# Five sevens in a row in the output product, and sums of the down weights at a period of seven steps

## The chip, the core and the metric

The kernel runs on one core of a Trainium2 chip. TensorE (PE) multiplies matrices, VectorE (DVE) and ScalarE (ACT) work on tiles in the core's memory, SyncE (SP) issues the transfers between DRAM and that memory; each engine works through its own list of instructions in order and waits on semaphores that others raise. The metric is device time in microseconds (us) of one execution: median of three runs 1462.11 us, from 1461.22 to 1462.31.

## The reference

One layer of a transformer for 256 tokens of width 2048: three kinds of attention heads, whose merged outputs go through `w_out` (2048 x 2048), and a feed-forward part whose up product has two halves of 5632 columns, each put through a causal convolution of width 3. All in float32.

```python
for l in range(DEPTH):
    h = rms_norm(x, g_mix[l])
    proj = h @ w_in[l]
    ...
    merged = (g[:, :, 0] * (o_fox @ w_br_fox[l])
              + g[:, :, 1] * (o_sb @ w_br_sb[l])
              + g[:, :, 2] * (o_mem @ w_br_mem[l]))
    x = x + merged @ w_out[l]

    h2 = rms_norm(x, g_ffn[l])
    u = causal_depthwise_conv(h2 @ w_up[l], conv_w[l], conv_b[l])
    u_gate, u_val = jnp.split(u, 2, axis=-1)
    x = x + (jax.nn.silu(u_gate) * u_val) @ w_down[l]
return x
```

The three attention branches stand in place of "..."; the change touches the products with `w_out`, `w_up` and `w_down`.

## The kernel before

Weights stream through the core in pieces of 128 x 1024 floats (512 KB). ScalarE casts each raw piece to a rounded part `hi`, VectorE subtracts to get the rest `lo`, and a product is the sum of three matmuls: x-hi by w-hi, x-lo by w-hi, x-hi by w-lo (`three`; in the up stage a matmul of 512 columns with both parts of x and one of 256 columns, L1231 and L1232). `hi` and `lo` have four buffers each, raw pieces four and, in some stages, two more.

The output and down stages (`blocked`) go through blocks of 1024 output columns. A block is a sum over pairs of 128-row slices of the weights: eight pairs in the output stage. A plan, a string, gives each pair's way:

- "e", `eight`: two slices by two halves of the tokens by two halves of the columns, eight products, 24 matmuls of 512 columns, two raw pieces.
- "s", `seven`: the same product of 2 x 2 blocks by seven products, 21 matmuls. It needs four sums of the activations (`pair_sums`, tiles `ms` in the output stage) and four sums of the weights, T1 to T4. Its loads are half a slice with T3, a whole slice, T1 with T2 as one piece (`raw_t`), and T4 (half a piece): 3.5 pieces.

The weights' sums don't depend on the activations, so they are made earlier in the kernel and kept in DRAM (`kept`). The list `halves` gives the order: the output stage's pairs first, then those of the down stage. Three streams draw from it: one in the attention stage (13 pairs, period 6), one by halves in the merged stage, and one in the up stage (`pair_sums_ahead`: period 8, sums one step behind the load, store five steps behind, starting after 22 steps). A step is one `tick`; the up stage ticks once for each piece of `w_up`. A pair of the stream is one load of 1 MB (`pre_d`), three additions on VectorE (`sums_in`, L249 to L251) and one store of 1 MB, all through one staging tile of tag "ends"; a new load waits until the last store has read the tile.

The up stage works on groups of four column tiles (`f0` = 0, 4, 8, ...; both halves `s` = 0 and 1 in turn). A group is eight pieces (`k` = 0, 2, ..., 14), 64 pairs of matmuls, into four banks. When a group is done, its four banks go through `conv` beside the next group: ScalarE copies half of a bank (L1167), VectorE adds the other half (L1168), scales it into one of two padded tiles (L1177), ScalarE applies one tap (L1182), VectorE two (L1183, L1184), and in the second half multiplies with the first half's result (L1190) and splits (L176, L177). On VectorE the pieces' `lo` are pinned to the order of the program by `pin`, the three additions by `in_order`; the convolution's rows are placed among them by a scheduler, which also sees the priorities that the program's order gives. One group of instructions on VectorE and ScalarE thus reads, as `lo_u24_0_6`, "lo of column tiles 24 to 27, half 0, slices 6 and 7".

## Time and profile before

| | |
|---|---|
| median of three runs | 1462.11 us (1461.22 to 1462.31) |
| the profiled execution | 1461.49 us, of which the span of its instructions 1459.8 |
| TensorE busy | 1454.0 us (100%), 7314 matmuls |
| VectorE busy | 1213.4 us (83%) |
| ScalarE busy | 850.0 us (58%) |
| output stage | 658 to 743 us of the span |
| up stage | 745 to 1225 us of the span |

The page's first part gives busy time per engine; the list of waits gives idle time of one engine by what it waited for; the chain goes back from the last instruction, at each step to what released it; windows give the same busy times for a stretch; timelines list single instructions with start, duration, engine, line, output and inputs, and in brackets the idle time ahead of them with what ended it. `x2` behind a row means two like instructions in one row. A duration includes a part in which the next instruction already runs: the spacing of starts is the pace.

### The profile page before, as it was taken

Reading aid. Unit: us, or ns where it says so; the run is one execution under the profiler, and the core shown is the slowest. Engines: PE = TensorE matmul, PEld = TensorE weight load, DVE = VectorE, ACT = ScalarE, POOL = GpSimd, SP = SyncE. Lnnn points to the kernel's source line nnn. Section 1 sums busy time; section 2 is a strip of 40 time slices with the busy share of each in tenths; the row PEclk is TensorE's granted clock in tenths of the full one; section 3 lists DMA queues with packets and bytes.
Section 4 is the critical chain, followed back from the end, with each engine's and each line's share of the span. In section 5 each row is a group of like instructions: output and inputs, shape, how many; then the busy total and the mean of one; then the engine's idle time right before and its main releaser. Section 6 shows DMA issues by size and latency. Waiting matters only on the chain.

```text
span 1459.8 us, 20547 instructions
## 1 busy us (share of the span) xinstructions
PE 1454.0 (100%) x7314; PEld 1230.1 (84%) x7314; DVE 1213.4 (83%) x1791; ACT 850.0 (58%) x1212; POOL 19.3 (1%) x48
## 2 busy tenths in 40 slices
PE   9999999999999999999999999999999999999998
PEld 7888888888888888888888888888888888888887
DVE  5778777776898899997887888888888877999878
ACT  6755454564564555545666556556556565676665
POOL 0000000010000000000000000000000000000000
PEclk9999999999999999999999999999999999999999
DMA  9697798777668576788877888888888866899995
GB/s 312 202 330 248 267 341 288 238 241 222 209 207 269 172 231 198 270 265 263 276 196 232 288 266 306 278 273 299 283 281 298 267 200 202 253 291 333 299 324 222
DMA packets 162534, 381.08 MB, mean 261 GB/s; under 512 B 12234, under 2 KB 27486, under 8 KB 158334
## 3 DMA queue, kind: packets, MB, share of 16 engines
q1 hardware_dynamic: 161022, 377.52, 78.9%
q10 hardware_dynamic: 1328, 2.11, 0.4%
q8 instruction: 57, 0.93, 0.3%
q14 instruction: 47, 0.39, 0.1%
q0 software_dynamic: 80, 0.13, 0.0%
HBM read 343.01 MB, written 36.70 MB: 260 GB/s over the span
## 4 chain that ended last, share of the span: by engine, by line
PE 97%; DVE 1%; DMA 1%; issue 0%; SPq 0%; ACT 0%; DVEq 0%; ACTq 0%
PE u L1231 22%; PE u L1232 11%; PE xd L329 3%; PE xd L330 3%; PE xd L328 3%; PE xg L330 3%; PE xg L329 3%; PE xg L328 3%; PE s L328 2%; PE s L330 2%; PE f L330 2%; PE f L328 2%; PE f L329 2%; PE s L329 2%; PE b L330 2%; PE b L328 2%
## 5 line engine op out<-in xcount | busy, mean ns | idle before, releaser
L1231 PE MATMUL u<-hT,hi_u 128*128 128x512 f32 x1232 | 428.3, 394 | 0.0
L1232 PE MATMUL u<-hT,lo_u 128*128 128x256 f32 x1232 | 341.3, 277 | 0.0
L1231 PEld LDWEIGHTS u<-hT,hi_u 128*128 128x128 f32 x1232 | 231.0, 188 | 53.8
L143 DVE TENSOR_TENSOR lo_u<-raw_u,hi_u 128x1024 fp32r<-128x1024 f32 x176 | 215.1, 1222 | 73.2 <-ACT hi_u L142 71.9
L142 ACT CAST hi_u<-raw_u 128x1024 fp32r<-128x1024 f32 x176 | 184.7, 1050 | 135.0 <-PE u L1231 106.7
L1232 PEld LDWEIGHTS u<-hT,lo_u 128*128 128x128 f32 x1232 | 231.2, 188 | 0.0
L323 DVE TENSOR_TENSOR lo_d<-raw_d,hi_d 128x1024 fp32r<-128x1024 f32 x88 | 106.7, 1222 | 16.2 <-ACT hi_d L322 13.8
L322 ACT CAST hi_d<-raw_d 128x1024 fp32r<-128x1024 f32 x88 | 91.7, 1053 | 38.8 <-PE xd L329 17.8
L322 ACT CAST hi_g<-raw_g 128x1024 fp32r<-128x1024 f32 (+1 forms) x80 | 77.1, 972 | 48.9 <-PE xg L329 19.2
L323 DVE TENSOR_TENSOR lo_g<-raw_g,hi_g 128x1024 fp32r<-128x1024 f32 (+1 forms) x80 | 88.6, 1119 | 4.1 <-ACT hi_g L322 4.1
L142 ACT CAST hi_f<-raw_f 128x1024 fp32r<-128x1024 f32 (+1 forms) x40 | 38.5, 967 | 51.8 <-PE f L329 42.8
L330 PE MATMUL xg<-lo_g,xT 128*128 128x512 f32 x175 | 68.1, 389 | 0.0
L329 PE MATMUL xg<-hi_g,xT 128*128 128x512 f32 x175 | 68.1, 389 | 0.0
L328 PE MATMUL xg<-hi_g,xT 128*128 128x512 f32 x175 | 68.1, 389 | 0.0
L143 DVE TENSOR_TENSOR lo_f<-raw_f,hi_f 128x1024 fp32r<-128x1024 f32 (+1 forms) x40 | 44.6, 1118 | 22.3 <-ACT hi_f L142 21.7
L143 DVE TENSOR_TENSOR lo_s<-raw_s,hi_s 128x1024 fp32r<-128x1024 f32 (+1 forms) x40 | 44.7, 1117 | 20.9 <-ACT hi_s L142 20.9
L1231 PE MATMUL u<-hT_rest,hi_u 128*128 128x512 f32 x176 | 62.0, 394 | 0.0
L142 ACT CAST hi_b<-raw_b 128x1024 fp32r<-128x1024 f32 x32 | 33.6, 1051 | 45.2 <-DMA raw_b<-in_w_br_fox_dram 15.8
L142 ACT CAST hi_s<-raw_s 128x1024 fp32r<-128x1024 f32 (+1 forms) x40 | 38.4, 961 | 36.8 <-PE s L329 23.9
L1182 ACT ACTIVATE y<-u,taps 128x256 f32<-128x256 f32 x88 | 49.6, 596 | 16.3 <-DVE u L1177 16.2
L330 PE MATMUL xd<-lo_d,aT 128*128 128x512 f32 x148 | 57.6, 389 | 0.0
L328 PE MATMUL xd<-hi_d,aT 128*128 128x512 f32 x148 | 57.6, 389 | 0.0
(520 smaller groups left out, 3473.1 us busy)
## 6 DMA issues: line engine op xcount, KB each, us to landing
raw_u<-in_w_up_dram SPq DMA_DIRECT2D x176, 512.0 KB, 4.5
raw_g<-in_w_in_dram SPq DMA_DIRECT2D x96, 512.0 KB, 4.4
raw_d<-in_w_down_dram SPq DMA_DIRECT2D x63, 512.0 KB, 5.4
pre_d<-in_w_down_dram SPq DMA_DIRECT2D x17, 1024.0 KB, 6.2
kept_d<-pre_d SPq DMA_DIRECT2D x17, 1024.0 KB, 6.2
raw_f<-in_w_in_dram SPq DMA_DIRECT2D x32, 512.0 KB, 4.9
raw_s<-in_w_in_dram SPq DMA_DIRECT2D x32, 512.0 KB, 5.2
raw_t_d<-kept_d SPq DMA_DIRECT2D x25, 512.0 KB, 5.8
```

What stands on the lines that cost most here:

```text
L142: pin(nc.scalar.copy(hi[:, :m], raw[:, :m]))
L143: pin(nc.vector.tensor_tensor(lo[:, :m], raw[:, :m], hi[:, :m].bitcast(F32), ALU.subtract))
L322: nc.scalar.copy(hi[:, :n], src)
L323: nc.vector.tensor_tensor(lo[:, :n], src, hi[:, :n].bitcast(F32), ALU.subtract)
L328: fix(nc.tensor.matmul(o, lhsT=ah, rhs=w[0], start=first, stop=False))
L329: fix(nc.tensor.matmul(o, lhsT=al, rhs=w[0], start=False, stop=False))
L330: fix(nc.tensor.matmul(o, lhsT=ah, rhs=w[1], start=False, stop=last))
L1182: nc.scalar.activation(y, u[:, 2:], AF.Identity, scale=tap(2), bias=tap(3))
L1231: nc.tensor.matmul(ps[i], lhsT=hi[:, j, c], rhs=hT(k + j), start=first, stop=False)
L1232: nc.tensor.matmul(ps[i][:, :S], lhsT=lo[:, j, c], rhs=hT(k + j)[:, :S], start=False, stop=last)
```

## The change

Four things change together. The output stage's plans go from two eights, two sevens, one eight, two sevens, one eight to two eights, five sevens, one eight. Before, the sevens took pairs 0 to 3 and the eights 4 to 7; now the five sevens take pairs 0, 1, 2, 3 and 6 and the eights 4, 5 and 7. The activations' sums for pair 6 are made by a new generator, `last_merged_sums`, in a tile of the tag under which the heads' outputs lay. Two more pairs of `w_out` stand at the front of `halves`, so two pairs of the down stage go from the attention stage's stream to the up stage's, which now makes 19 and goes at period 7, with the sums in the step of the load and the store four steps behind. And the up stage's matmuls are pinned to the program's order.

```diff
-    o_plans = ("eessesse", "eessesse")
+    o_plans = ("eessssse", "eessssse")
...
+    o_sevens = (0, 1, 2, 3, 6)
+    pairs = lambda name, n: o_sevens if name == "o" else range(n)
...
-        for pr in range(plan.count("s"))
+        for pr in pairs(name, plan.count("s"))
...
-        s, e = 0, ns
+        s, e = 0, 0
+        sp = pairs(name, ns)
+        ep = [p for p in range(len(plan) - plan.count("f")) if p not in sp]
...
-                by_seven(s, s == 0, s == ns - 1)
+                by_seven(sp[s], s == 0, s == ns - 1)
...
-                eight(e, i == 0, i == len(plan) - 1)
+                eight(ep[e], i == 0, i == len(plan) - 1)
...
     def merged_sums():
         yield 1
-        for p in range(o_plans[0].count("s")):
+        for p in range(4):
...
+    def last_merged_sums():
+        yield 2
+        after = op.tile([P, KT, 2 * S], F32R, tag="ot", name="m_after")
+        ms[6] = after[:, 0:2].rearrange("p k c -> p (k c)").rearrange("p (f l q) -> p f l q", f=4, l=2)
+        pair_sums(mT[6], block("mw_6"), [(ms[6], slice(0, 4))])
...
+    later(last_merged_sums())
...
-        pair_sums_ahead(lambda name: ends_tile(name, F32).rearrange("p i c -> p (i c)"), 8, 1, 5, delay=DU)
+        pair_sums_ahead(lambda name: ends_tile(name, F32).rearrange("p i c -> p (i c)"), 7, 0, 4, delay=DU)
...
-                        nc.tensor.matmul(ps[i], lhsT=hi[:, j, c], rhs=hT(k + j), start=first, stop=False)
-                        nc.tensor.matmul(
-                            ps[i][:, :S], lhsT=lo[:, j, c], rhs=hT(k + j)[:, :S], start=False, stop=last
+                        in_order(nc.tensor.matmul(ps[i], lhsT=hi[:, j, c], rhs=hT(k + j), start=first, stop=False))
+                        in_order(
+                            nc.tensor.matmul(
+                                ps[i][:, :S], lhsT=lo[:, j, c], rhs=hT(k + j)[:, :S], start=False, stop=last
+                            )
```

In the changed kernel the lines behind line 236 have other numbers: L249 to L251 are L251 to L253, L1168 is L1179, L1177 is L1188, L1183 and L1184 are L1194 and L1195, L1190 is L1201, L384 is L386, L415 to L421 are L417 to L423.

What the order shows, at three places. First SyncE's queue in block 0 of the output stage: `raw_o0_5` is slice 5 of the weights, the second of pair 2; `raw_t_o0_2` is pair 2's T1 and T2, `raw_t4_o0_2` its T4. Before:

```order
L419 DMA raw_t_o0_1_6102<-kept_o0_1_1030 128x2x512
L384 DMA raw_o0_13_6161<-in_w_out_dram 128x1024
L421 DMA raw_t4_o0_2_6186<-kept_o0_2_1201 128x512
L415 DMA raw_o0_4_6179<-in_w_out_dram 128x512
L416 DMA raw_o0_4_6179<-kept_o0_2_1201 128x512
L384 DMA raw_o0_5_6182<-in_w_out_dram 128x1024
L419 DMA raw_t_o0_2_6184<-kept_o0_2_1201 128x2x512
```

and now:

```order
L421 DMA raw_t_o0_1_6102<-kept_o0_1_1030 128x2x512
L386 DMA raw_o0_5_6154<-in_w_out_dram 128x1024
L423 DMA raw_t4_o0_2_6158<-kept_o0_2_1201 128x512
L421 DMA raw_t_o0_2_6156<-kept_o0_2_1201 128x2x512
L417 DMA raw_o0_6_6197<-in_w_out_dram 128x512
L418 DMA raw_o0_6_6197<-kept_o0_3_1392 128x512
```

The pieces of the eight (12, 13) no longer stand between pairs 1 and 2; the first piece of pair 2 is issued far earlier (not shown), and its T load is three rows behind that of pair 1 instead of six.

Second, VectorE in the up stage behind `lo_u12_0_4`, the piece of column tiles 12 to 15, half 0, slices 4 and 5; `cr`, `u`, `y` and `aT` are tiles of the convolution of tiles 8 to 11. Before:

```order
L143 TENSOR_TENSOR lo_u12_0_4_8181<-raw_u12_0_4_8179,hi_u12_0_4_8180 128x1024
L1168 TENSOR_TENSOR cr_8_1_8113<-cr_8_1_8113,u8_1_7864 128x256
L1168 TENSOR_TENSOR cr_9_1_8124<-cr_9_1_8124,u9_1_7865 128x256
L1177 TENSOR_TENSOR u_0_6990<-cr_8_1_8113,rbc_5954 128x256
L1177 TENSOR_TENSOR u_1_6992<-cr_9_1_8124,rbc_5954 128x256
L143 TENSOR_TENSOR lo_u12_0_6_8203<-raw_u12_0_6_8201,hi_u12_0_6_8202 128x1024
L1183 TENSOR_SCALAR y_8_1_8117<-u_0_6990,taps_110,y_8_1_8117 128x256
```

Now the row of `lo_u12_0_4` is followed by 27 others, 24 of the convolution and the three sums, until `lo_u12_0_6`; the last twelve rows from there:

```order
L252 TENSOR_TENSOR pre_d0_10_8231<-pre_d0_10_8231 128x512
L1194 TENSOR_SCALAR y_10_1_8190<-u_0_7018,taps_110,y_10_1_8190 128x256
L1194 TENSOR_SCALAR y_11_1_8201<-u_1_7020,taps_110,y_11_1_8201 128x256
L1195 TENSOR_SCALAR y_10_1_8190<-u_0_7018,taps_110,y_10_1_8190 128x256
L1195 TENSOR_SCALAR y_11_1_8201<-u_1_7020,taps_110,y_11_1_8201 128x256
L1201 TENSOR_TENSOR y_10_0_7963<-y_10_0_7963,y_10_1_8190 128x256
L1201 TENSOR_TENSOR y_11_0_7972<-y_11_0_7972,y_11_1_8201 128x256
L253 TENSOR_TENSOR pre_d0_10_8231<-pre_d0_10_8231 128x512
L177 TENSOR_TENSOR aT_6749<-y_10_0_7963,aT_6749 128x256
L177 TENSOR_TENSOR aT_6749<-y_11_0_7972,aT_6749 128x256
L143 TENSOR_TENSOR lo_u12_0_6_8238<-raw_u12_0_6_8236,hi_u12_0_6_8237 128x1024
```

Before, four rows stood between the two lo pieces; now the whole convolution of the four banks does, with a pair's sums among it. Like runs stand behind `lo_u24_0_6` (18 rows of the convolution and the sums), `lo_u24_1_4` (16) and `lo_u28_0_2` (17).

Third, the last of these, VectorE behind `lo_u28_0_2`. Before:

```order
L143 TENSOR_TENSOR lo_u28_0_2_9953<-raw_u28_0_2_9951,hi_u28_0_2_9952 128x1024
L143 TENSOR_TENSOR lo_u28_0_4_9997<-raw_u28_0_4_9995,hi_u28_0_4_9996 128x1024
L1168 TENSOR_TENSOR cr_24_1_9929<-cr_24_1_9929,u24_1_9680 128x256
L1168 TENSOR_TENSOR cr_25_1_9940<-cr_25_1_9940,u25_1_9681 128x256
L1177 TENSOR_TENSOR u_0_6990<-cr_24_1_9929,rbc_5954 128x256
```

and now:

```order
L143 TENSOR_TENSOR lo_u28_0_2_9989<-raw_u28_0_2_9987,hi_u28_0_2_9988 128x1024
L251 TENSOR_TENSOR pre_d1_8_10010<-pre_d1_8_10010 128x1024
L252 TENSOR_TENSOR pre_d1_8_10010<-pre_d1_8_10010 128x512
L1179 TENSOR_TENSOR cr_24_1_9965<-cr_24_1_9965,u24_1_9716 128x256
L1179 TENSOR_TENSOR cr_25_1_9976<-cr_25_1_9976,u25_1_9717 128x256
L1188 TENSOR_TENSOR u_0_7018<-cr_24_1_9965,rbc_5954 128x256
```

Here two of the sums come directly behind the lo piece, the convolution of tiles 24 to 27 behind them, and `lo_u28_0_4` behind that.

## Prediction

> **What bounds the kernel now.** I read the page's shares first, then the waits of TensorE, then windows by stage, and last the timelines of VectorE and TensorE in the two stages that the change touches. Page, parts 1 and 4:

> ```profile
> span 1459.8 us, 20547 instructions
> PE 1454.0 (100%) x7314; PEld 1230.1 (84%) x7314; DVE 1213.4 (83%) x1791; ACT 850.0 (58%) x1212; POOL 19.3 (1%) x48
> PE 97%; DVE 1%; DMA 1%; issue 0%; SPq 0%; ACT 0%; DVEq 0%; ACTq 0%
> ```

> All waits of TensorE (line waited for; us in total, times, longest):

> ```profile
> PE spare L92 <- DVE qscale L531: 1.2, 1, 1.2
> PE kv L154 <- DVE memT L185: 0.5, 2, 0.2
> ```

> Both lie in the first microseconds. So the time is the sum of the matmuls: every matmul taken away shortens it, and every microsecond by which a piece of weights is late lengthens it. The windows below are the output stage, the up stage without its ends, and a piece of the down stage with five sevens in a row (busy time of each engine, granted clock, DMA share, GB/s):

> ```profile
> 658.00:743.20 85.20, 85.20 (x390) 70.75 (x389) 70.25 (x80) 53.65 (x69) 0.00 (x0) 1.00 0.82 260
> 780.00:1200.00 420.00, 420.00 (x2425) 367.17 (x2424) 361.43 (x595) 252.33 (x389) 0.00 (x0) 1.00 0.84 276
> 1421.00:1444.50 23.50, 23.50 (x106) 19.42 (x105) 20.14 (x20) 18.30 (x21) 0.00 (x0) 1.00 0.90 326
> ```

> TensorE fills each window. VectorE is 86% busy in the up stage (361.43 of 420): room on average, but only if its work comes evenly.

> **Part 1, the products.** Per block of the output stage one eight (24 matmuls) becomes a seven (21), so 6 matmuls of 512 columns go. Their spacing, from two rows that are 14 matmuls apart:

> ```profile
> 739.79 0.39 PE L328 MATMUL xo<-hi_o,mT 128*128 128x512 f32 x1
> 742.97 0.39 PE L330 MATMUL xo<-lo_o,mT 128*128 128x512 f32 x1
> ```

> 3.18 / 14 = 0.227 us each, hence **−1.36 us** (0.09%). Changes under 0.2%, 2.9 us, can hardly be told from none on this kernel; by itself this term would read as the same.

> **Part 2, five sevens in a row.** A seven brings 3.5 pieces per 21 matmuls where an eight brings 2 per 24. The third window shows the denser stream (326 GB/s, share 0.90) carried for 23.5 us without a gap on TensorE, so I cost the rate at nothing. The one transfer that moves to a tighter place is the T load of pair 2 in block 0: two pieces of an eight no longer stand ahead of it. It takes the raw slot that came free at 674.33; its nearest like, issued at 677.08, landed when its cast started at 683.33, 6.25 us later:

> ```profile
> 674.33 0.33 SPq L415 DMA_DIRECT2D raw_o<-in_w_out_dram  x1
> 677.08 0.38 SPq L419 DMA_DIRECT2D raw_t_o<-kept_o  x1
> 679.49 1.06 ACT L322 CAST hi_o<-raw_o 128x1024 fp32r<-128x1024 f32 x1 [0.30 <-PE yo L329]
> 683.33 1.05 ACT L322 CAST hi_t_o<-raw_t_o 128x1024 fp32r<-128x1024 f32 x1 [1.52 <-DMA raw_t_o<-kept_o]
> 690.78 1.83 DVE L323 TENSOR_TENSOR lo_t_o<-raw_t_o,hi_t_o 128x1024 fp32r<-128x1024 f32 x2
> 693.58 0.39 PE L330 MATMUL yo<-lo_t_o,ms 128*128 128x512 f32 x1
> ```

> 674.33 + 6.25 = 680.6, against the cast slot at 679.49: 1.1 late. The reserve is 1.57 us (lo done 692.01, read 693.58). Cost 0, bounds 0 and 1.1. Pair 6's own sums (five VectorE rows, some 2.3 us by the like operations below) fall in VectorE's idle time, the times in brackets:

> ```profile
> 668.05 1.23 DVE L323 TENSOR_TENSOR lo_t_o<-raw_t_o,hi_t_o 128x1024 fp32r<-128x1024 f32 x1 [1.33 <-ACT hi_t_o L322]
> 670.81 0.69 DVE L323 TENSOR_TENSOR lo_t_o<-raw_t_o,hi_t_o 128x512 fp32r<-128x512 f32 x1 [0.94 <-PE mt L989]
> 673.07 1.23 DVE L323 TENSOR_TENSOR lo_o<-raw_o,hi_o 128x1024 fp32r<-128x1024 f32 x1 [0.93 <-ACT hi_o L322]
> ```

> Those are 3.2 us in one stretch of six. Without that cover the sums could delay the lo pieces behind them by up to 2.3, of which the 1.57 of reserve takes most: under 1 us, inside the range.

> **Part 3, the up stage.** TensorE's order does not change here; VectorE's does. A piece of w_up takes eight pairs of L1231 and L1232, 22.2 / 8 = 2.77 us. One column group is eight pieces. At period 8 the sums of a pair (L249 to L251) keep one place in the group, behind the last lo piece, clear of the conv work. At period 7 they come one piece earlier each time, and at four pairs they run into the conv rows; there the whole run now stands ahead of a lo piece. The prices:

> ```profile
> 920.93 1.23 DVE L143 TENSOR_TENSOR lo_u<-raw_u,hi_u 128x1024 fp32r<-128x1024 f32 x1 [1.55 <-ACT hi_u L142]
> 922.10 0.77 DVE L1168 TENSOR_TENSOR cr<-cr,u 128x256 f32<-128x256 f32 x2
> 923.70 1.23 DVE L143 TENSOR_TENSOR lo_u<-raw_u,hi_u 128x1024 fp32r<-128x1024 f32 x1 [0.16 <-ACT hi_u L142]
> 924.84 0.87 DVE L1183 SCALAR_TENSOR_TENSOR y<-u,taps,y 128x256 f32<-128x256 f32 x2
> ...
> 928.77 1.22 DVE L143 TENSOR_TENSOR lo_u<-raw_u,hi_u 128x1024 fp32r<-128x1024 f32 x1
> 936.51 1.22 DVE L249 TENSOR_TENSOR pre_d<-pre_d 128x1024 f32<-128x1024 f32 x1
> 937.64 0.42 DVE L177 TENSOR_TENSOR aT<-y,aT 128x256 fp32r<-128x256 f32 x1
> 937.98 0.69 DVE L250 TENSOR_TENSOR pre_d<-pre_d 128x512 f32<-128x512 f32 x1
> 938.58 1.22 DVE L143 TENSOR_TENSOR lo_u<-raw_u,hi_u 128x1024 fp32r<-128x1024 f32 x1
> ```

> Starts give the pace: 11 conv operations from 924.84 to 928.77 are 0.357 us each. A pair's sums are 1.13 (936.51 to 937.64) + 0.60 (937.98 to 938.58) and, with the same form as L250, 0.60 again: 2.33 us. And how far ahead of TensorE a lo piece is:

> ```profile
> 922.53 0.39 PE L1231 MATMUL u<-hT,hi_u 128*128 128x512 f32 x1
> 930.86 0.39 PE L1231 MATMUL u<-hT,hi_u 128*128 128x512 f32 x1
> 931.09 0.27 PE L1232 MATMUL u<-hT,lo_u 128*128 128x256 f32 x1
> ```

> By tile numbers the lo of 923.70 is first read at 931.09, and the one of 920.93 (done 922.16) one piece, 2.77 us, before. So from the end of one lo to the need of the next there are 931.09 − 922.16 = 8.93 us, and the next lo itself takes 1.22: **7.71 us of other work fit between two lo pieces**. What the new order puts there, counted row by row:

> - A, behind lo of f12, first half, k = 4: 24 conv operations and the sums, 24 × 0.357 + 2.33 = 10.9: 3.2 late.
> - B, behind f24, first half, k = 6: 18 and the sums, 8.76: 1.05 late.
> - C, behind f24, second half, k = 4: 16 and the sums, 8.04: 0.33 late.
> - D, behind f28, first half, k = 2: 17 and the sums, 8.40: 0.7 late. Here the first two sums (1.73 us) stand right behind the lo, would end in this group at 919.38 + 1.73 = 921.1, and the first conv must wait for ScalarE's copy of the finished bank, whose first half the conv at 922.10 took: 1.0 more, 1.7.

> ```profile
> 918.15 1.23 DVE L143 TENSOR_TENSOR lo_u<-raw_u,hi_u 128x1024 fp32r<-128x1024 f32 x1 [0.68 <-ACT hi_u L142]
> 921.69 0.73 ACT L1167 COPY cr<-u 128x256 f32<-128x256 f32 x2 [0.79 <-PE u L1232]
> ```

> Sum **+6.3 us**, bounds 0 (if the lead is longer than in this group) and 9.3 (if the conv work of A, B and C waits 1.0 for ScalarE's copy too, as in D). Before, the worst run between two lo pieces was the 11 operations shown, 3.93 us, which is why nothing waits. What is late next after a stall is nothing: casts go on behind free buffers while TensorE stands.

> **Part 4, transfers of the stream.** One staging tile serves the pairs in turn: load, sums, store, next load. Issue to landing, by part 6 of the page:

> ```profile
> raw_u<-in_w_up_dram SPq DMA_DIRECT2D x176, 512.0 KB, 4.5
> pre_d<-in_w_down_dram SPq DMA_DIRECT2D x17, 1024.0 KB, 6.2
> kept_d<-pre_d SPq DMA_DIRECT2D x17, 1024.0 KB, 6.2
> ```

> Load and store are 12.4 us of 7 × 2.77 = 19.4 (before 22.2): 7.0 us remain for the sums to get done, against 9.8. Where they stand behind 8.6 us of conv work, the store slips, the next load waits on SyncE's queue, and the raw_u loads behind it wait too; with 0.84 of the DMA engines' time taken and two pairs (4 MB each way) more to move, it catches up slowly. No row shows such a slip. Bounds: 0, since raw_u lies four buffers ahead, and 5, if each of A to D hands on its whole 8.6 − 7.0 = 1.6 us with a little less. I take **1.3**, nearer to the lower end because the buffers cover a single slip of 1.6.

> **The sum.** 1461.49 − 1.36 + 6.3 + 1.3 = 1467.7 us against the profiled execution. The median of the runs stands 0.62 above that execution, so 1468.3.

> **Rivals.**
> 1. *The stalls don't come.* For it: VectorE is 14% idle, and a lead of 6.2 us is measured in one group. It decides where the work between two lo pieces stays under 7.7 us; if the lead were 11 us (the length of A), nothing would wait, and 1461.49 − 1.36 + 0.62 = 1460.8, not slower. Against it: the lead is capped by four lo buffers, and four pieces at 2.77 us are 11.1 from which the cast, the subtract and the matmuls' own use of a buffer are off. A weaker form, with A alone late, gives 1464.0.
> 2. *Transfers bind.* The slips of part 4 add up from pair to pair: 19 pairs, of which five or six hand on 1.6 us: 4 to 8 more than the forecast, 1472 to 1476. For it: DMA share 0.84, and one tile for all. Against: the third window above moved 326 GB/s, 18% more than the up stage's 276.
> 3. *The clock falls behind the longest stall.* At the program's start seven spare matmuls of 384 columns take 2.42 us, 0.346 each, twice what the spacing above gives, until about 3.8 us after the first. At the end the last matmul ends at 1455.83, and the granted clock is 1.00 up to 1459 and lower behind it:

> ```profile
> 1.23 2.42 PE L92 MATMUL spare<-idle 128*128 128x384 bf16 x7 [1.23 <-DVE qscale L531]
> 1455.55 0.28 PE L330 MATMUL apart<-lo_d,a_ends 128*128 128x256 f32 x1
> 1458.00:1459.00 1.00, 0.00 (x0) 1.00 0.00 0
> 1459.00:1459.80 0.80, 0.00 (x0) 0.56 0.04 10
> ```

> So an idle time of over 3.2 us can halve the clock for some 3.8 us, which loses half of that, 1.9 us. A is at that edge: 1470.2. [...]
> 4. *The output stage starves* with five sevens in a row: about 1 us per block, 1470.3. Against: the third window.

> That six matmuls go is certain from the order; the rest of the output stage's plan only changes places.

> **How the numbers follow.** Forecast 0.64 (1465.5 to 1471.5), rival 1 in full 0.07, in its weaker form 0.08, rival 2 0.13, rival 3 0.05, rival 4 0.03. The range 1463 to 1475.5 leaves out rival 1 in full and the top of rival 2. Faster by over 0.2% needs a gain that no row shows: 0.03. Within 0.2% are rival 1 and most of its weaker form: 0.14. Slower: 0.83.

> **What the profile after would show.** TensorE waits for VectorE's lo_u in the list of waits, in four places: about 3 us at f12, 1 to 2 at f24 and f28. VectorE's busy time stays within 10 us of before; the spacing of matmuls is unchanged; the output stage's last matmul comes 1.4 us earlier than before. If TensorE has no waits in the up stage, part 3 is wrong; if the waits name a transfer of raw_u, rival 2 is right; a granted clock under 1.00 between 780 and 1200 is rival 3.

## The result, and the profile after

The changed kernel takes 1476.11 us (median of five, 1473.42 to 1479.24), the kernel before 1461.61 beside it: a ratio of 1.0098, 95% interval 1.0084 to 1.0112. It is slower, as forecast, but by 14.5 us where 6.2 were expected, and 0.6 us above the range. One thing is new beside the median: the five runs spread over 5.8 us, those of before over 1.1. The profiled execution is the quickest of the five.

The page after, parts 1 and 4:

```profile
span 1471.7 us, 20604 instructions
PE 1459.3 (99%) x7308; PEld 1234.1 (84%) x7308; DVE 1222.2 (83%) x1806; ACT 854.4 (58%) x1217; POOL 19.3 (1%) x48
PE 93%; DVE 3%; DMA 2%; issue 1%; ACT 0%; SPq 0%; DVEq 0%; ACTq 0%
```

Six matmuls fewer, yet TensorE is *busy* 5.3 us longer (1459.3 against 1454.0), and the span is 11.9 longer. So only a part of the loss is waiting; the rest is matmuls that take longer. The list of TensorE's waits (line waited for; us in total, times, longest):

```profile
PE u L1244 <- DVE lo_u L143: 6.6, 4, 3.7
PE spare L92 <- DVE qscale L535: 1.2, 1, 1.2
```

Four waits for `lo_u`, 6.6 us. The chain has 3% of VectorE and 2% of DMA where before had 1% of each: at these waits it goes back from TensorE over VectorE's rows to the transfers of the one staging tile. Windows of the changed kernel with TensorE alone (busy us, matmuls, granted clock, DMA share, GB/s), the up stage and then the time around the longest wait:

```profile
780.00:1200.00 420.00, 413.42 (x2359) 0.99 0.81 282
887.00:891.50 4.50, 0.81 (x6) 0.80 0.27 117
891.50:896.50 5.00, 5.00 (x16) 0.50 0.98 341
896.50:901.50 5.00, 5.00 (x30) 1.00 1.02 377
```

Behind the wait TensorE is busy for 5 us at a granted clock of 0.50 and does 16 matmuls where 30 would fit.

The longest wait, first TensorE and then VectorE of the changed kernel:

```profile
887.32 0.40 PE L1242 MATMUL u<-hT,hi_u 128*128 128x512 f32 x1
891.41 0.58 PE L1244 MATMUL u<-hT,lo_u 128*128 128x256 f32 x1 [3.69 <-DVE lo_u L143]
```

```profile
877.18 1.23 DVE L143 TENSOR_TENSOR lo_u<-raw_u,hi_u 128x1024 fp32r<-128x1024 f32 x1 [0.54 <-ACT hi_u L142]
878.38 0.78 DVE L1179 TENSOR_TENSOR cr<-cr,u 128x256 f32<-128x256 f32 x2
...
880.61 1.23 DVE L251 TENSOR_TENSOR pre_d<-pre_d 128x1024 f32<-128x1024 f32 x1 [0.77 <-DMA pre_d<-in_w_down_dram]
...
889.47 0.76 DVE L177 TENSOR_TENSOR aT<-y,aT 128x256 fp32r<-128x256 f32 x2
890.14 3.49 DVE L143 TENSOR_TENSOR lo_u<-raw_u,hi_u 128x1024 fp32r<-128x1024 f32 x3
```

Between the lo of 877.18 and the next at 890.14 stand the 24 rows of the convolution and the sums, with 0.77 us in which VectorE waits for the load of the pair whose sums come next. The chain shows why that load is late: it could start only when the store of the pair before had left the tile (start, us, what).

```profile
866.82 6.43 DMA kept_d<-pre_d
873.26 7.25 DMA pre_d<-in_w_down_dram
880.61 1.23 DVE pre_d L251
```

At 890.14 three lo pieces follow at once: the casts were long done.

Beside these waits there is a second, quieter loss. From f8, k = 10 to the first wait, and from f36, k = 10 to the end of the stage, a piece takes 2.827 us instead of 2.773, at a granted clock of 1.00 and without a wait in the list: 0.0533 us a piece, 6.7 ns for each pair of matmuls. The slow stretch begins where a lo piece was in time by a hair, first VectorE's piece, then TensorE's reading of it:

```profile
846.52 1.22 DVE L143 TENSOR_TENSOR lo_u<-raw_u,hi_u 128x1024 fp32r<-128x1024 f32 x1
```

```profile
847.98 0.28 PE L1244 MATMUL u<-hT,lo_u 128*128 128x256 f32 x1
848.10 0.40 PE L1242 MATMUL u<-hT,hi_u 128*128 128x512 f32 x1
```

Done at 847.74, read 0.24 us later; the piece at f36, k = 10 was ready 0.24 us ahead as well. The slow pace is not new, though: in the kernel before, too, the first two pieces of the up stage go at it, until sixteen transposes (L196) interrupt the stream.

```profile
743.53 0.40 PE L1231 MATMUL u<-hT,hi_u 128*128 128x512 f32 x1
748.12 0.40 PE L1231 MATMUL u<-hT,hi_u 128*128 128x512 f32 x1
```

```profile
751.28 0.39 PE L1231 MATMUL u<-hT,hi_u 128*128 128x512 f32 x1
758.22 0.39 PE L1231 MATMUL u<-hT,hi_u 128*128 128x512 f32 x1
```

Ahead of the transposes these are 13 pairs in 4.59 us, 353 ns each, and behind them 20 pairs in 6.94 us, 347 ns each. All fourteen profiles of this case begin the up stage so.

Between the changed kernel's waits the pace is again that of before; TensorE from 900 to 1000 us, of before and of the changed kernel:

```profile
900.00:1000.00 100.00, 100.00 (x579) 1.00 0.86 290
```

```profile
900.00:1000.00 100.00, 100.00 (x579) 1.00 0.85 296
```

Added up from the starts of TensorE's matmuls (spacing over the regular 0.232 us), for the profile and for a second one of the same kernel, against the profile of before:

| us | first profile | second profile |
|---|---|---|
| before the output stage | +1.2 | +0.7 |
| output stage | −1.1 | −0.7 |
| waits A, B, C, D | 3.86, 1.11, 0.57, 1.67 = 7.2 | 4.45, 2.15, 0.58, 1.67 = 8.9 |
| matmuls at the low clock behind them | 2.4 | 4.3 |
| pieces at 2.827 us | 2.1 | 1.4 |
| the first matmuls behind each wait | 0.3 | 0.3 |
| last matmul, in all | 12.3 | 14.8 |

(The rounded terms add to 12.1 and 14.9.) The first line is not put down to the change: among the profiles of versions that leave the stages ahead as they are, with and without the five sevens, the output stage begins 0.1 us earlier to 1.8 us later than in that of before.

### The profile page after: what moved, and what is told of

It reads as the page before. It is cut to its first block, busy times and chain, and to the rows that moved or that the text cites. A ratio compares the mean times of both kernels' runs of the same rounds, so it can differ in the third digit from the quotient of the medians.

```text
span 1471.7 us, 20604 instructions
## 1 busy us (share of the span) xinstructions
PE 1459.3 (99%) x7308; PEld 1234.1 (84%) x7308; DVE 1222.2 (83%) x1806; ACT 854.4 (58%) x1217; POOL 19.3 (1%) x48
## 4 chain that ended last, share of the span: by engine, by line
PE 93%; DVE 3%; DMA 2%; issue 1%; ACT 0%; SPq 0%; DVEq 0%; ACTq 0%
PE u L1242 20%; PE u L1244 11%; PE xg L332 4%; PE xg L330 4%; PE xg L331 4%; PE xd L331 3%; PE xd L330 3%; PE xd L332 3%; PE s L330 2%; PE s L332 2%; PE f L332 2%; PE f L330 2%; PE f L331 2%; PE s L331 2%; PE b L330 2%; PE b L331 2%
## 5 line engine op out<-in xcount | busy, mean ns | idle before, releaser
L1244 PE MATMUL u<-hT,lo_u 128*128 128x256 f32 x1232 | 346.0, 281 | 6.6 <-DVE lo_u L143 6.6
L143 DVE TENSOR_TENSOR lo_u<-raw_u,hi_u 128x1024 fp32r<-128x1024 f32 x176 | 213.2, 1220 | 78.9 <-ACT hi_u L142 78.2
L142 ACT CAST hi_u<-raw_u 128x1024 fp32r<-128x1024 f32 x176 | 184.6, 1050 | 149.0 <-PE u L1242 90.4
L324 ACT CAST hi_d<-raw_d 128x1024 fp32r<-128x1024 f32 x88 | 91.8, 1054 | 40.9 <-PE xd L331 14.9
L142 ACT CAST hi_f<-raw_f 128x1024 fp32r<-128x1024 f32 (+1 forms) x40 | 38.6, 967 | 51.3 <-PE f L331 46.3
L330 PE MATMUL xg<-hi_g,xT 128*128 128x512 f32 x175 | 68.1, 389 | 0.0
L143 DVE TENSOR_TENSOR lo_s<-raw_s,hi_s 128x1024 fp32r<-128x1024 f32 (+1 forms) x40 | 44.6, 1117 | 21.4 <-ACT hi_s L142 21.4
L143 DVE TENSOR_TENSOR lo_f<-raw_f,hi_f 128x1024 fp32r<-128x1024 f32 (+1 forms) x40 | 44.5, 1117 | 21.4 <-ACT hi_f L142 20.7
L142 ACT CAST hi_s<-raw_s 128x1024 fp32r<-128x1024 f32 (+1 forms) x40 | 38.4, 961 | 36.9 <-PE s L331 25.4
L142 ACT CAST hi_b<-raw_b 128x1024 fp32r<-128x1024 f32 x32 | 33.7, 1053 | 44.1 <-PE b L331 19.6
L331 PE MATMUL xd<-hi_d,aT 128*128 128x512 f32 x148 | 57.6, 389 | 0.0
L330 PE MATMUL xd<-hi_d,aT 128*128 128x512 f32 x148 | 57.6, 389 | 0.0
## 6 DMA issues: line engine op xcount, KB each, us to landing
raw_u<-in_w_up_dram SPq DMA_DIRECT2D x176, 512.0 KB, 5.2
raw_g<-in_w_in_dram SPq DMA_DIRECT2D x96, 512.0 KB, 4.5
raw_d<-in_w_down_dram SPq DMA_DIRECT2D x63, 512.0 KB, 5.5
pre_d<-in_w_down_dram SPq DMA_DIRECT2D x19, 1024.0 KB, 7.4
kept_d<-pre_d SPq DMA_DIRECT2D x19, 1024.0 KB, 5.0
raw_f<-in_w_in_dram SPq DMA_DIRECT2D x32, 512.0 KB, 4.8
raw_s<-in_w_in_dram SPq DMA_DIRECT2D x32, 512.0 KB, 5.2
raw_t_d<-kept_d SPq DMA_DIRECT2D x25, 512.0 KB, 5.7
```

What stands on the lines that cost most here:

```text
L142: pin(nc.scalar.copy(hi[:, :m], raw[:, :m]))
L143: pin(nc.vector.tensor_tensor(lo[:, :m], raw[:, :m], hi[:, :m].bitcast(F32), ALU.subtract))
L324: nc.scalar.copy(hi[:, :n], src)
L330: fix(nc.tensor.matmul(o, lhsT=ah, rhs=w[0], start=first, stop=False))
L331: fix(nc.tensor.matmul(o, lhsT=al, rhs=w[0], start=False, stop=False))
L1244: nc.tensor.matmul(ps[i][:, :S], lhsT=lo[:, j, c], rhs=hT(k + j)[:, :S], start=False, stop=last)
```

## The experiments

Rivals at this point: the sums' place among VectorE's rows (theory), the two more pairs' transfers, the five sevens themselves, the pinning of the matmuls; and for what the waits leave behind, chance or a rule of their length.

**The additions left out.** The sums are not made in the up stage; loads and stores stay at period 7, so the down stage's weights are not summed there.

```diff
-                if t == add:
+                if t == add and not delay:
                     sums_in(w)
```

> The changed kernel with the three additions of each pair left out in the up stage alone: loads and stores go at period 7 as changed, so the down stage multiplies with unsummed weights there. If the additions among the convolution's rows make the four waits, none is left, the pace is 2.773 throughout, and the time is that of before less the six matmuls: 1460 to 1461.5, which also clears the 19 pairs' transfers at period 7. If the transfers make lo pieces late, the waits stay: 1468 or more.

Measured 1460.69 us (ten runs, nine of them 1459.5 to 1460.9 and one 1470.1) against 1462.14; ratio 0.9995, interval 0.9982 to 1.0007. In its profile the up stage has no wait and the old count of matmuls:

```profile
780.00:1200.00 420.00, 420.00 (x2425) 1.00 0.84 286
```

The output stage is 1.35 us shorter, where 1.36 were forecast. So nineteen pairs at period 7 move without harm, at 286 GB/s in this window against 276; the three additions make the waits. The single run at 1470.1 fits what two experiments below show.

**The stream without the output stage.** The kernel before, with the new period and the pinning alone.

```diff
-        pair_sums_ahead(lambda name: ends_tile(name, F32).rearrange("p i c -> p (i c)"), 8, 1, 5, delay=DU)
+        pair_sums_ahead(lambda name: ends_tile(name, F32).rearrange("p i c -> p (i c)"), 7, 0, 4, delay=DU)
...
+                        in_order(nc.tensor.matmul(ps[i], lhsT=hi[:, j, c], ...))
```

> The kernel before, with the up stage's stream at period 7, sums at once, store four steps behind, and its matmuls pinned to the program's order; the output stage as before, 17 pairs. My theory: the same four waits as in the changed kernel, 3.9, 1.1, 0.6 and 1.7 us, and what follows from them, so 1473 to 1478. If the two more pairs or the output stage are the cause: under 1464.

Measured 1476.72 us, ratio 1.0105 (1.0092 to 1.0118), 1474.24 to 1480.77:

```profile
PE u L1233 <- DVE lo_u L143: 6.5, 4, 3.6
```

The same four waits without a change in the output stage. Its profile differs from the changed kernel's mainly in the pace: behind the wait at f24 all pieces to the end of the stage take 2.827 us.

**Without the pinning.**

```diff
-                        in_order(nc.tensor.matmul(ps[i], lhsT=hi[:, j, c], rhs=hT(k + j), start=first, stop=False))
+                        nc.tensor.matmul(ps[i], lhsT=hi[:, j, c], rhs=hT(k + j), start=first, stop=False)
```

> The changed kernel without the pinning of the up stage's matmuls. In the program built so, TensorE takes matmuls with the rounded part for other column tiles ahead of the late rest at three places. [...] If the pinning is neutral: 1476.

Measured 1473.04 us (1.0072, 1.0057 to 1.0086; 1468.48 to 1474.63), waits 4.0 us in three (2.7 the longest). So the scheduler, left free, puts some matmuls ahead of a late piece and saves 2.6 us of waiting; the pinning is a part of the loss. The clock fell here too: behind a wait of 2.86 us by spacing it was at 0.50 for 2.9 us of work.

```profile
891.60:894.50 2.90, 2.73 (x10) 0.50 0.95 322
```

**The old period, begun earlier.**

```diff
-        ..., 7, 0, 4, delay=DU)
+        ..., 8, 1, 5, delay=6)
```

> The changed kernel with the up stage's stream at its old steps (period 8, sums one step behind the load, store five), and begun after 6 steps instead of 22 so that its 19 pairs still fit; everything else as changed. If the loss comes from sums of weights that walk through the convolution's rows on VectorE (my theory), TensorE has no wait in the up stage, its pace there is 2.77 us per piece throughout, and the time is that of before less the six matmuls: 1460.5, between 1460 and 1461.5. If it comes from two more pairs' transfers (19 loads and stores of 1 MB), the waits stay and the time is 1465 or more. If five sevens in a row or pair 6's sums cost something, the output stage is longer than the 1.1 us shortening that the changed kernel shows there.

A miss: 1464.84 us, ratio 1.0035 (1.0019 to 1.0052). From 815 us on there is no wait, but the stream now begins in the first groups, and TensorE waits there: 0.25, 0.40, 1.03 and 1.22 us by spacing, between 786 and 815. The chain to the second and third of these is one of transfers (start, us, what):

```profile
764.58 14.61 DMA kept_d<-pre_d
779.27 0.37 SPq L303
779.74 8.64 DMA raw_u<-in_w_up_dram
788.48 1.06 ACT hi_u L142
```

A store of the stream takes 14.6 us here, where the page of before has 6.2 at the median. SyncE's queue waits 9.8 us for it before it can issue the next load of the stream; a load of a piece of `w_up` stands behind that in the queue, and its cast comes too late for TensorE. The first wait, too, lies behind a cast that waited 3.7 us for its load; ahead of the last one a pair's sums stand among the convolution's rows again. So in these groups the transfers of the stream do delay `raw_u`, and this run doesn't separate the two causes as it was meant to; the run without the additions does. The twelve runs fall in two groups, seven from 1462.4 to 1465.1 and five from 1470.9 to 1473.1, with nothing between. That would be the size of the slow pace over all that follows the last wait: (1233 − 815) / 2.773 = 151 pieces by 0.0533 are 8.0 us. The profile is of the quicker group.

**One wait alone.** The kernel before (matmuls pinned, which leaves the order of every engine as it was), with one extra VectorE instruction ahead of one lo piece.

```diff
+        if name == "u8_0_12":
+            in_order(nc.vector.tensor_tensor(unused part of aT, 19 x 256, raw, hi, ALU.subtract))
```

> The kernel before, its up stage's matmuls pinned (the order of every engine is that of before), with one extra VectorE instruction of 19 x 256 elements ahead of the lo piece k = 12 at f8, first half: the first rung of the ladder alone, where TensorE waited 0.6 us. If a wait draws TensorE's pace for all that follows until the next wait, the runs fall in two groups: near 1462.7 (the wait alone) and near 1470.1 (the wait and 139 pieces at 2.827 instead of 2.773 us, 7.4 us), with nothing between. If the slow pace of the ladder and of the changed kernel has another cause (two more pairs, the period, several waits), all runs stay near 1462.7.

Nine runs from 1461.99 to 1463.80 and three from 1469.93 to 1470.34, nothing between (before: 1460.86 to 1463.52, median 1461.82). The profile caught one of the three. Its waits in the up stage, and then TensorE in windows ahead of and behind the place:

```profile
PE u L1242 <- DVE lo_u L150: 0.5, 1, 0.5
```

```profile
780.00:850.00 70.00, 70.00 (x405) 1.00 0.78 261
900.00:1000.00 100.00, 100.00 (x569) 1.00 0.86 293
1000.00:1200.00 200.00, 200.00 (x1135) 1.00 0.81 267
```

569 matmuls in 100 us, where the kernel before does 579, with TensorE busy throughout and the clock at 1.00. One added instruction thus costs the half microsecond of its wait in most executions, and 7.6 more in some. Here the pace changed six pieces behind the wait, where no wait is listed. The lo piece there, k = 8 of f8's second half, was again in time by a hair, done at 868.19 and read at 868.44:

```profile
866.97 1.22 DVE L152 TENSOR_TENSOR lo_u<-raw_u,hi_u 128x1024 fp32r<-128x1024 f32 x1
868.44 0.28 PE L1242 MATMUL u<-hT,lo_u 128*128 128x256 f32 x1
```

In all profiles together the pace changes for good, behind 780 us and without a wait just ahead, nine times, and each time at a piece that was ready only 0.15 to 0.27 us before it was read. Not every such piece changes it.

**Ladders of waits.** Twelve such instructions in one execution, 19 to 30 and, in a second kernel, 16 to 33 times 256 elements; one run of each, 1504.99 and 1507.41 us.

> The kernel before with its up stage's matmuls pinned and one extra VectorE instruction of known length put ahead of the lo piece k = 12 at twelve groups (f8 to f28, both halves): 19, 20, 21, 22, 23, 24, 25, 26, 28, 30, 24 and 22 times 256 elements, about 5.1 to 8.1 us. By my reading of the lead (a lo piece starts 7.4 us before it is read, of which the subtract takes 1.2) TensorE should wait from about 6 us on, by what is over: 0 at the first three, up to 2.2 at the tenth. Theory of the pace (from the changed kernel, where TensorE goes from 2.773 to 2.827 us per piece behind two places where a lo was in time by only 0.3 us): such a step shows behind the rungs that are within 0.3 us of the edge, and goes back behind a longer wait. Rival: the pace depends on the transfers or on the time in the program, then the rungs change nothing in it.

> The ladder again with other lengths, so that most waits come between 2 and 3 us: 25, 24, 16, 26, 19, 31, 18, 33, 18, 31, 17 and 23 times 256 elements. In the runs so far waits up to 1.95 us left the granted clock alone, those of 2.86 and more were all followed by 2.4 to 4.9 us at half the clock, and one of 2.15 was. Theory 1 (an idle time of some length halves the clock): there is an edge near 2.1 us and the waits of this run show it. Theory 2 (a window that runs freely): between 2 and 3 us some waits drop the clock and others don't, without an edge. Pace behind each wait: 2.773 or 2.827, and no rule by the wait's length.

The lead was less than expected: the first ladder's waits began at its first rung. The lengths are read from the starts of TensorE, so this doesn't touch the rest. Waits of 0.40 us and more of all profiles in order of length, with the pace behind them and the time that TensorE worked at the low clock:

| wait, us | clock behind it | pace behind it |
|---|---|---|
| 0.40 to 1.85 (twenty-three) | stays | slow behind ten, 2.773 behind twelve, and behind four of these slow later on; the shortest has no stretch of its own |
| 2.15 | low 3.4 us | 2.773 |
| 2.24 | stays | 2.773 |
| 2.78, 2.81 | stays | slow |
| 2.86 | low 2.9 us | slow |
| 2.98 to 5.47 (thirteen) | low 3.2 to 5.6 us, 1.5 to 2.6 lost | slow behind four, else 2.773 |

The pace shows no rule by length in these waits. For the clock theory 2 holds: by the length of the wait alone there is no edge, and behind 2.15 it was low where behind 2.81 it stayed. The traces also show the window. In the second ladder the low clock begins at 880.25, 955.34, 982.64, 1033.85 and 1088.46 us, which are 22, 8, 15 and 16 times 3.413 us apart, and it lasts one or two such lengths; the first three:

```profile
880.25:883.66 3.41, 3.41 (x12) 0.50 0.88 265
955.34:958.75 3.41, 3.15 (x10) 0.50 0.56 156
982.64:989.47 6.83, 5.45 (x17) 0.50 0.59 178
```

In the changed kernel's first profile the low clock lasts from 889.70 to 896.53 us, 6.83 or two such lengths, and TensorE was busy for 1.43 us in the 3.41 ahead of it. So the changes of the granted clock seen here lie on a grid of 3.41 us, and what goes with a fall is how short TensorE was busy in the window that ends there. The 2.15 of the changed kernel's second profile (1029.68 to 1031.83) lie almost wholly in one window and leave 1.43 us of work in it. The clock falls at its end, when TensorE has worked again for 1.35 us, and comes back one window later:

```profile
1029.76:1033.18 3.42, 1.43 (x9) 1.00 0.80 307
1033.18:1036.59 3.41, 3.41 (x12) 0.50 0.87 285
1036.59:1040.00 3.41, 3.41 (x21) 1.00 0.96 340
```

A wait of 2.65 (listed; 2.81 by spacing) in the second ladder lies across two windows of that execution's grid, which keep 2.56 and 1.61 us of work, and the clock stays at 1.00:

```profile
929.83 0.39 PE L1242 MATMUL u<-hT,lo_u 128*128 128x256 f32 x1 [2.65 <-DVE lo_u L150]
924.62:928.03 3.41, 2.56 (x15) 1.00 0.63 243
928.03:931.44 3.41, 1.61 (x9) 1.00 0.14 19
```

This separates all cases here. In the six profiles in which the clock falls inside the up stage, with the grid laid through the first fall, TensorE was busy for 0 to 1.43 us in each of the 15 windows that end with a fall, and for 1.61 us or more in every other window at the full clock between 20 and 1450 us. At the low clock, it came back behind windows with 2.85 us of work or more and stayed low behind those with 2.18 or less.

**The changed kernel again.**

> The changed kernel once more, for a second profile. If the pace behind a wait is drawn anew at each, the same four waits stand at the same pieces with nearly the same lengths, the near-miss at f8 k = 10 may or may not set the slow pace, the stretches between the waits have other paces than in the first profile, and the time is 1461.5 + 9 to 10 (waits, clock, less six matmuls) + 0.053 us for each piece at the slow pace.

1475.97 us. The four waits stand at the same pieces, A and B longer (4.45 and 2.15): in B VectorE waited 0.95 us for ScalarE in the convolution, and for loads it waited 2.5 us in all instead of 1.7. The near-miss at f8 did not set the slow pace this time, and the clock fell twice. So these two executions differ by the lengths of the waits (7.2 and 8.9 us in all), by the low clock behind them (2.4 and 4.3), which hangs on where they fall on the grid, and by the pieces at the slow pace (2.1 and 1.4).

**Ways to keep the six matmuls.** Two versions move the two pairs into the stages ahead and put the up stage back row for row.

```diff
-        half_sums(..., 8, 2, 5, "merged")
+        half_sums(..., 5, 2, 4, "merged")
-        ..., 7, 0, 4, delay=DU)
+        ..., 8, 1, 5, delay=DU)
```

> The changed kernel with five sevens, but the two more pairs are made in the merged stage, whose stream by halves goes at period 5 (sums two steps, store four behind the load) instead of 8; the up stage's stream is back at period 8 with 17 pairs, and VectorE's order in the up stage is row for row that of before. Theory of the late lo pieces: no wait in the up stage, pace 2.773 throughout, and six matmuls less: 1460.5, and runs as close together as those of before. If period 5 makes lo pieces of the gates' products late, waits of TensorE at xg or yg appear between 360 and 660 us and eat the 1.1 to 1.4 us. If the five sevens alone bring a loss: over 1461.5 with waits in the output stage.

> As the run before, but one of the two pairs is made in the attention stage (14 pairs instead of 13) and the merged stage's stream goes at period 6 (store five behind): the additions spread thinner. Up stage as before again. Expected 1460.5; if the attention stage's last pair comes late at its end, up to 2 us of waits near 315 us, 1461 to 1463.

Both missed: 1467.73 (1.0038, 1.0026 to 1.0051) and 1464.41 (1.0017, 1.0008 to 1.0026). The up stage is as before (420.00 busy, x2425 in the window of the first), but the same thing happens one stage earlier, in the branches' products. Waits of the first there:

```profile
PE b L332 <- DVE lo_b L143: 3.2, 4, 1.3
PE yo L330 <- DVE mT L177: 0.8, 1, 0.8
```

The branches' products from 614 us on lost 4.4 us in the first and 1.5 in the second, and the output stage of the first, which the second line belongs to, is 2.0 us longer than without the additions. A third version shares the pairs out, 14 in the attention stage and 18 in the up stage at period 8:

```diff
-    background.append(pair_sums_ahead(in_turn, PF, 3, 7, most=13))
+    background.append(pair_sums_ahead(in_turn, PF, 3, 7, most=14))
-        ..., 7, 0, 4, delay=DU)
+        ..., 8, 1, 5, delay=DU)
```

> The changed kernel with the two more pairs shared out: 14 pairs instead of 13 in the attention stage at period 6, 18 instead of 17 in the up stage at period 8 (sums one step behind the load, store five, begun after 22 steps); the merged stage as before. The eighteenth pair is loaded two steps before the last group and finished at its start. By the theory of the late lo pieces, with the sums again at one place of each group: no wait in the up stage, except that the last pair's store may hold up raw_u loads at f40, and in the attention stage at most the 0.2 us that 14 pairs cost in the run before. Expected 1460.5 to 1461.5; at period 8 a slow pace (2.827) would need a wait first.

> The version with 14 pairs in the attention stage and 18 in the up stage, without the pinning of the up stage's matmuls; every engine's order is the same as with it. If the pinning has nothing to do with the slow pace, some of the runs are near 1470 to 1473 again and the rest at 1460 to 1462; if it has, all are at 1460 to 1462, and this version beats the kernel before by about 0.9 us.

Pinned 1461.23 us, unpinned 1461.08; ratios 1.0010 (0.9991 to 1.0029) and 1.0006 (0.9992 to 1.0019): no difference that can be told. Nine of twelve runs of the first lie between 1460.1 and 1462.7, ten of the second between 1460.2 and 1463.3, some 0.9 us under before; three and two lie between 1469.7 and 1473.4. The profile of the first caught one of these. It has no wait in the up stage; TensorE keeps the slow pace of the first two pieces behind the transposes, to the end:

```profile
780.00:1200.00 420.00, 420.00 (x2379) 1.00 0.84 277
```

2379 matmuls in a full window against 2425. From its first matmul (745.11) to its last (1244.22) the stage takes 9.3 us longer than before (743.20 to 1233.03). The order being the same with and without the pinning, both having such runs, the pinning isn't what draws the pace. Neither version beats the kernel before.

## Why the prediction was right or wrong

- *TensorE bounds the time, late lo pieces lengthen it, the four places and their lengths:* right. Forecast 3.2, 1.05, 0.33 and 1.7 us, listed 3.69, 0.95, 0.42 and 1.51 in the profile. That they come from the sums is shown by the run without them. A's excess is covered by the 0.77 us for which the sums waited for their own load; part 4 had sought such a delay on SyncE's queue.
- *Six matmuls, −1.36:* right where nothing else disturbs (−1.35 without the sums); in the profiles with an unchanged merged stage up to 0.7 of it was lost again in the output stage, inside the bounds given.
- *Pinning:* costed at nothing, since TensorE's order does not change by it. That was wrong: without it the scheduler's order for the changed stream is another one, 2.6 us of waiting better.
- *Part 4, transfers, 1.3 us, and rival 2:* in the changed kernel TensorE waits for no `raw_u`, and without the sums the same transfers cost nothing. The mechanism itself, a late store that holds up the queue, came in the run with the stream begun earlier. Two pairs are 2 MB each way, not the 4 that part 4 has; no sum uses it. The part of the range above 1472 rested on this, and the time lies there for other reasons.
- *"What is late next after a stall is nothing":* **this is the step that failed.** It priced a stall at its length; two things came on top here. First, the clock fell: rival 3 had the fall and its price (1.9 us; measured 1.4 to 2.6) but a chance of 0.05, since the threshold of over 3.2 us was read from one row, the end of the kernel, and A from a sum that came out at that edge. (The slow matmuls at the program's start are no second row: the profile gives the granted clock as 1.00 there.) It fell behind all thirteen waits from 2.98 us on, one of 2.86 and one of 2.15; what separates these from the others is the work left in a window of 3.41 us, at most 1.43 us against 1.61 or more. Second, behind some of the waits and near-misses the pace was 2.827 us a piece instead of 2.773. That was in no term and no rival, and "the spacing of matmuls is unchanged" stood among the signs. The first 5 us of the up stage of before show the slow pace, but the window read there began at 780. It is worth 2.1 us in the first profile, and up to 139 × 0.0533 = 7.4 us, from f8 to the end of the stage, where every draw is slow; that is enough for the spread of the five runs, of which one was profiled.
- *The sum:* 1467.7 was set against the profiled 1473.4. Of the 5.7 missing, 0.9 are waits, 2.4 the clock, 2.1 the pace, 1.2 the start and the gates, 0.3 the output stage and 0.3 the matmuls behind the waits, less the 1.3 for transfers: 5.9. The median stands 2.7 above the profiled execution; other draws would do that, but no profile of those runs shows it.
- The words on the kernel say that the lo pieces are pinned by `pin`. In the up stage they are not: the switch behind it is off from L744 on, and of VectorE's work there only the sums and four rows of the first group are kept in order. That leaves the scheduler free to put a whole run of the convolution ahead of a lo piece, as the order shows.

## What to carry to other kernels

A stream of extra work whose period doesn't divide the loop it runs beside walks through every phase of that loop; count the work between two deadlines at each phase, not the average load. In these runs a stall of TensorE could cost more than its length: one that left TensorE 1.43 us of work or less in a window of the 3.41 us grid also cost 1.4 to 2.6 us of low clock, and whether a stall between 2 and 3 us did so hung on where it fell (2.15 and 2.86 us did, 2.24, 2.78 and 2.81 didn't). Where times of one kernel fall into two groups, compare counts of matmuls in equal windows with TensorE fully busy. A profile of one execution, the quickest by chance, can hide a part of such a loss.

## What was not expected of the hardware

TensorE showed two paces for the same stream of matmuls, 346.7 and 353.3 ns a pair of 512 and 256 columns, at a granted clock of 1.00. In these profiles it held one until the stream was interrupted, by a wait or by the transposes, or until a piece was ready only 0.15 to 0.27 us ahead. Which pace followed was not to be told from a wait's length (0.40 to 5.47 us). Of 78 runs of the kernel before beside these experiments none was over 1464.4 us, though in its profile, too, the stage begins slow and turns at the transposes, while 6 of 34 runs of the three versions without a further wait there were near 1470 or above. What protects it, and what makes the pace, stays open: no view names a resource for it.
